# Compressing keys and values by pairs of taps over all 128 rows, with the positions' share prepared in layer 0

## The chip, the cores and the metric

The kernel runs on one core of a Trainium2 chip. The metric is the device time of one execution in microseconds (us); lower is better.

## The reference

Two layers of a decoder trunk on 256 tokens of width 1024: layer 0 mixes tokens by two sparse attentions, layer 1 by an attention with three branches; each layer then has cross-attention into 256 memory tokens and a SwiGLU feed-forward part. The change is about one small part of layer 1's mixer, the compressed branch:

```python
def nsa_compress(x, pos_emb, w1, w2):           # x: (1, 256, 4 groups, 64)
    n_cmp = (S - 32) // 16 + 1                  # 15 blocks
    idx = jnp.arange(n_cmp)[:, None] * 16 + jnp.arange(32)[None, :]
    blk = x[:, idx] + pos_emb[None, None, :, None, :]
    blk = blk.transpose(0, 1, 3, 2, 4).reshape(B, n_cmp, G, 32 * 64)
    return jax.nn.silu(blk @ w1) @ w2
...
    kc = rms_norm(nsa_compress(grp(kc), pos_k, w1_k, w2_k), kcmp_norm)
    vc = nsa_compress(grp(vc), pos_v, w1_v, w2_v)
```

Block n of a group covers tokens 16n to 16n+31, so it has 32 taps, each a vector of 64. Each tap has its own 64 x 64 slice of w1. The position embedding adds the same vector to all blocks: pos @ w1, 64 numbers for the keys and 64 for the values.

## The kernel before

Tokens lie in two tiles of 128 rows (t = 0, 1). All large weights are split in two fp32r halves: a raw tile of 2 x 128 rows by up to 512 columns comes by DMA from SyncE's queue (three raw buffers, `RAWS`), ScalarE or VectorE writes the high half (`move`), VectorE the low half (the `tensor_tensor` in `pusher`), both into one of six `whl` buffers (`PAIRS`). Such a pair is called a unit below. A raw buffer is filled anew when its unit has been split. TensorE takes three matmuls per product (`mm3`); the last multiplication of the feed-forward part, `fo`, uses each unit for 12 matmuls of 512 columns (2 tiles t x 2 row blocks x 3), and goes through 22 units, fo0 to fo21, accumulating in four PSUM tiles (`mm` and `po`).

The order of instructions on every engine is made when the program is built. Parts of the work are generators; `Steps` takes the next operation of the generators in the order of times that `Est`, the planner, gives them, and a lower rank goes first among operations that could start within 0.03 us. `Est` has a clock for each engine. What it knows of a transfer is what `est.note` tells it: `load` moves its clock of the queue by 1.45 us for a load of 512 columns and lets it land 2.0 us later. A matmul is taken for ready 0.5 us after its operands (`SLACK`). On the chip each engine goes through its instructions in that order and waits at each for its operands.

`load_cmp` is spawned by `ffn(0)` when all of the feed-forward part but `fo` has been given out. It takes four slots of the 36 shared places and issues twelve DMAs on SyncE's queue (eight of 128 KB for w1, two for w2, two for the positions, tile `posemb`). It tells the planner of none of them. Nothing in layer 0 reads them.

In layer 1, `ev_kc` transposes the four groups of keys and values of a tile on TensorE, so that the 64 dimensions of the keys stand in partitions 0 to 63 and those of the values in 64 to 127, and copies the result to `kvT`, token by token. `prep` transposes the positions and puts them in `kvT` as a fifth group. `compress` then runs 32 taps; a tap is two fp32 matmuls, one for keys and one for values, each 64 rows by 64 columns of weights, in opposite corners of the array, with 75 moving columns (5 groups x 15 blocks, 16 tokens apart). After every eight taps (`TAPS`) it waits in the planner's order for another matmul step. The positions' column of the result, `pb`, is the bias of the following silu. The rest of `compress` ends with `done("cmp")`, for which `attention` waits.

Tensors in the profile: `kvT` the transposed keys and values; `place` any of the shared places (w1, the feed-forward activations aT, scores, and others); `posemb` the positions; `w` is w2; `tp`, `sp`, `mm`, `po` are PSUM. Every operation of an engine is recorded on line 252, a helper. An fp32 matmul leaves two records, an fp32r matmul one.

Of the kernel before, what the change touches and what calls it, by code (L numbers as in the profile page):

```python
# [8 lines left out]
F32 = mybir.dt.float32  # L9
F32R = mybir.dt.float32r  # L10
# [5 lines left out]
P = 128  # L16
NB = 4
# [71 lines left out]
class Steps:  # L89
# [7 lines left out]
    def spawn(self, g, rank=2):  # L97
        self.n += 1
        self.new.append([rank, self.n, g, None])
# [253 lines left out]
def trunk(ctx: ExitStack, tc: tile.TileContext, I, out):  # L353
# [28 lines left out]
    def tt(o, a, b, op):  # L382

        return either(V.tensor_tensor(o, a, b, op=op), PO.tensor_tensor(o, a, b, op=op))
# [19 lines left out]
    def done(k):  # L404
        flags[k] = flags.get(k, 0) + 1

    def has(k, n=1):
        return lambda: flags.get(k, 0) >= n

    def tiny(n, name="tiny"):  # L410
        return tp.tile([P, n], F32, name=name, tag="tiny", bufs=96)
# [630 lines left out]
    w1s = {}  # L1042

    def load_cmp():
        w2 = hp.tile([P, P], F32, name="w2")
        pos = hp.tile([32, P], F32, name="posemb")
        yield PO.memset(w2, 0.0)
        w1 = []
        for j in range(4):
            w = yield from SL.get([P, 8, HD])  # L1050
            w1.append(w)
            for i, s in enumerate("kv"):
                nc.sync.dma_start(w[0][64 * i:64 * i + 64],
                                    I[f"nsa_cmp_w1_{s}"][0, 512 * j:512 * j + 512].rearrange("(t d) h -> d t h", d=HD))
        for i, s in enumerate("kv"):
            nc.sync.dma_start(w2[64 * i:64 * i + 64, 64 * i:64 * i + 64], I[f"nsa_cmp_w2_{s}"][0])
            nc.sync.dma_start(pos[:, 64 * i:64 * i + 64], I[f"nsa_cmp_pos_{s}"][0])
        w1s.update(w1=w1, w2=w2, pos=pos)
        done("cmpw")

    def mixer1():
# [1 line left out]
        kT = {}  # L1063
        vv = hp.tile([P, NT, 8, HD], F32, name="vv", tag="v8")
        gt = [hp.tile([P, G * HG, 3], F32, name=f"gt{t}") for t in range(NT)]
        kvT = hp.tile([P, G + 1, SEQ], F32, name="kvT", tag="kvT")
        kbd = hp.tile([P, G, 2, NCMP], F32, name="kbd")
        rq = {(j, t): hp.tile([P, 8], F32, name=f"rq{j}{t}") for j in range(2) for t in range(NT)}
        vbig = {}

        def prep():
            yield has("cmpw")
            yield PO.memset(kvT[:, G, 32:], 0.0)
            ps, f = yield from TP.get([P, 512])
            yield T.transpose(ps[:, :32], w1s["pos"], ident[:32, :32])
            yield V.tensor_copy(kvT[:, G, :32], ps[:, :32])
            f()
            done("kvT")

        def ev_kc(ps, free, t):  # L1080
            c, cf = yield from T2.get([P, G, 2, HD])
            yield S.activation(c, ps.rearrange("p (b g d) -> p g b d", b=2, g=G), AF.Copy, scale=(yield from root("mix1", t))[1])
            free()
            tps, f = yield from TP.get([P, 512])
            for g in range(G):
                yield T.transpose(tps[:, g * P:(g + 1) * P], c[:, g].rearrange("p a d -> p (a d)"), ident)
            yield S.activation(kvT[:, :G, t * P:(t + 1) * P], tps.rearrange("p (a b) -> p a b", a=G), AF.Copy)
            f()
            cf()
            done("kvT")  # L1090

        def compress():
            yield has("kvT", 3)
            NB = (G + 1) * NCMP
            N = G * NCMP
            w1 = w1s["w1"]
            hps, hf = yield from PV.get([P, 512])
            for tt in range(32):
                if tt % TAPS == 0 and tt:
                    yield has("mm", flags["mm"] + 1)  # L1100
                for i in range(2):
                    yield T.matmul(hps[64 * i:64 * i + 64, :NB], w1[tt // 8][0][64 * i:64 * i + 64, tt % 8, :],
                             kvT[64 * i:64 * i + 64, :, tt:tt + 16 * (NCMP - 1) + 1:16],
                             start=(tt == 0), stop=(tt == 31), tile_position=(64 * i, 64 * i))
            for w in w1:
                w[1]()
            pb = tiny(1, "pb")
            yield V.tensor_copy(pb, hps[:, N:N + 1])
            hs = tp.tile([P, N], F32, name="hs")
            yield S.activation(hs, hps[:, :N], AF.Silu, bias=pb)  # L1110
            hf()
            cps, f = yield from TP.get([P, 512])
            yield T.matmul(cps[:N, :P], hs, w1s["w2"], start=True, stop=True)
            kc2 = tp.tile([N, 2, HD], F32, name="kc2")
            vc = tp.tile([N, HD], F32, name="vc")
            yield V.tensor_copy(vc, cps[:N, HD:P])
            sq = tp.tile([P, HD], F32, name="sqc", tag="sqk", bufs=2)
            ss = tiny(1, "ssc")
            yield S.activation(sq[:N], cps[:N, :HD], AF.Square, accum_out=ss[:N])
            yield V.tensor_scalar(ss[:N], ss[:N], 1.0 / HD, EPS, op0=OP.mult, op1=OP.add)  # L1120
            rk = tiny(1, "rkc")
            yield from pow_half(rk[:N], ss[:N])
            yield V.tensor_scalar(kc2, cps[:N, None, :HD].to_broadcast([N, 2, HD]), rk[:N], None, op0=OP.mult)
            f()
            yield PO.memset(kbd, 0.0)
            kps, f = yield from TP.get([P, 512])
            yield T.transpose(kps[:, :N], kc2.rearrange("p a b -> p (a b)"), ident[:N, :N])
            for i in range(2):
                yield V.tensor_scalar(kbd[64 * i:64 * i + 64, :, i, :],
                                kps[64 * i:64 * i + 64, :N].rearrange("p (g n) -> p g n", g=G),  # L1130
                                kv[64 * i:64 * i + 64, 4:5], None, op0=OP.mult)
            f()

            M = 8 * NCMP
            for j in range(2):
                vbig[j] = yield from SL.get([P, 8, HD])
                vb = vbig[j][0]
                sel = tp.tile([N, 2, HG, NCMP], F32, name="sel", tag="sel")
                yield PO.memset(sel, 0.0)
                yield PO.affine_select(sel, sel, pattern=[[-NCMP, 2], [0, HG], [-1, NCMP]], compare_op=OP.not_equal,  # L1140
                                 fill=1.0, base=-2 * j * NCMP, channel_multiplier=1)
                vps, f = yield from TP.get([P, 512])
                yield T.matmul(vps[:M, :HD], sel.rearrange("p a b c -> p (a b c)"), vc, start=True, stop=True)
                vt = tp.tile([M, HD], F32, name="vt", tag="vt")
                yield V.tensor_copy(vt, vps[:M, :HD])
                f()
                yield PO.affine_select(vb[:M], vt[:, None, :].to_broadcast([M, 8, HD]),
                                 pattern=[[-NCMP, 8], [0, HD]], compare_op=OP.is_ge, fill=0.0, base=0,
                                 channel_multiplier=1)
                yield PO.affine_select(vb[:M], vb[:M], pattern=[[NCMP, 8], [0, HD]], compare_op=OP.is_ge,  # L1150
                                 fill=0.0, base=NCMP - 1, channel_multiplier=-1)
            done("cmp")
# [157 lines left out]
                                    kT[e, g][1]()  # L1310

        h = [hsel(t) for t in range(NT)]
        spawn(prep())
        spawn(compress())
        spawn(attention())
        for t in range(NT):
# [44 lines left out]
        return lambda k: tuple(mT[k // 2][e][0][:, k % 2, t * P:(t + 1) * P] for e in range(2))  # L1361

    def mem_k(L):
        kT = [hp.tile([P, MH, SEQ], F32R, name=f"mkT{e}") for e in range(2)]
        mkv[L, "k"] = kT

        def ev(ps, free, t):
            q, qf = yield from T2.get([P, MH, MD])
            yield S.activation(q.rearrange("p h d -> p (h d)"), ps, AF.Copy)
            rk = tiny(MH, "mrk")  # L1370
            yield has("mr", 1 + t)
            yield from inv_rms(ps, MH, MD, mvr[t][0], 1.0 / MD, 1.0, rk, free)
            yield V.tensor_tensor(q, q, rk[:, :, None].to_broadcast([P, MH, MD]), op=OP.mult)
            tps, f = yield from TP.get([P, 512])
            for i in range(MH):
                yield T.transpose(tps[:, i * P:(i + 1) * P], q[:, i, :], ident)
            tv = tps.rearrange("p (a b) -> p a b", a=MH)
            hi, lo = (kT[e][:, :, t * P:(t + 1) * P] for e in range(2))
            yield move(hi, tv, kv[:, 5 + L:6 + L])
            yield V.scalar_tensor_tensor(lo, tv, kv[:, 5 + L:6 + L], hi.bitcast(F32), op0=OP.mult, op1=OP.subtract)  # L1380
            f()
            qf()
            done(("mk", L))
        for t in range(NT):
            yield from gemm((L, "mk"), t, msel(t), KD, ev, pairs(("mT", L)))
# [253 lines left out]
```

## Time and profile before

| | |
|---|---|
| median of 3 runs | 785.92 us (784.57 to 786.65) |
| the profiled execution | 785.81 us |
| its span, first to last instruction | 784.0 us |
| TensorE busy | 757.2 us, 97% of the span |
| VectorE, ScalarE, GpSimd busy | 531.3, 435.7, 122.7 us |
| mean granted TensorE clock | 0.995 |

The profiled execution's own time is the span and 1.81 us around it. TensorE is busy in nearly all of the span; in the page's forty slices it is below 9 tenths in four of the first five (from 0 to 98 us) and in the last. TensorE's busy time says nothing about how fast its matmuls run.

### The profile page before, as it was taken

How to read it: one execution, taken by the hardware profiler on the slowest of the kernel's cores; microseconds unless marked ns; L12 is line 12 of the kernel's file. 1: busy time of each engine (PE TensorE's matmuls, PEld its weight loads, DVE VectorE, ACT ScalarE, POOL GpSimd, SP SyncE). 2: the span in 40 equal slices, each digit the busy share in tenths (PEclk: the TensorE clock that was granted, in tenths of full speed). 3: DMA queues.
4: the chain of work that ended last, by engine and by line, in shares of the span. 5: the costliest groups of instructions: out<-in, count | busy, mean ns of one | idle time of the engine just before them, and what ended most of it. 6: DMA issues, size and time to landing. Idle time of an engine off the chain costs nothing.

```text
span 784.0 us, 11770 instructions
## 1 busy us (share of the span) xinstructions
PE 757.2 (97%) x4227; PEld 629.6 (80%) x4227; DVE 531.3 (68%) x1111; ACT 435.7 (56%) x819; POOL 122.7 (16%) x169
## 2 busy tenths in 40 slices
PE   6898899999999999999999999999999999999998
PEld 5777687798888888878788787887888888889886
DVE  6899998778655545555717889978767546546542
ACT  5677786566545444344525889846656444444440
POOL 1554430210000000000106365301200000000000
PEclk9999899999999999999999999999999999999999
DMA  6735424435465554777524723034435566546761
GB/s 213 207 101 162 147 96 159 164 108 168 156 210 179 164 185 122 203 243 229 172 58 129 219 77 110 14 122 163 160 115 167 162 201 188 165 130 214 221 184 54
DMA packets 70635, 122.32 MB, mean 156 GB/s; under 512 B 8549, under 2 KB 15793, under 8 KB 70577
## 3 DMA queue, kind: packets, MB, share of 16 engines
q1 hardware_dynamic: 70544, 121.58, 49.7%
q8 instruction: 33, 0.54, 0.3%
q14 instruction: 26, 0.20, 0.1%
q0 software_dynamic: 32, 0.00, 0.0%
HBM read 120.51 MB, written 1.05 MB: 155 GB/s over the span
## 4 chain that ended last, share of the span: by engine, by line
PE 73%; DVE 10%; DMA 6%; ACT 4%; POOL 3%; issue 3%; SPq 1%; ACTq 0%; POOLq 0%; DVEq 0%
PE mm L252 56%; PE po L252 9%; PE tp L252 6%; DVE whl L252 3%; DMA raw<-in_ffn_w_out 3%; PE sp L252 3%; DVE place L252 3%; ACT whl L252 2%; ACT place L252 2%; DMA raw<-in_nsa_w_in 2%; POOL rope L252 1%; DMA raw<-in_ab_w_in 1%; POOL place L252 1%; DVE hss L252 1%; DMA raw<-in_nsa_w_out 1%
## 5 line engine op out<-in xcount | busy, mean ns | idle before, releaser
L252 PE MATMUL mm<-whl,h 128*128 128x512 f32 (+3 forms) x1776 | 400.4, 379 | 3.6 <-DVE whl L252 3.2
L252 DVE TENSOR_TENSOR whl<-raw,whl 128x1024 fp32r<-128x1024 f32 (+3 forms) x232 | 272.2, 1180 | 135.6 <-ACT whl L252 133.4
L252 PEld LDWEIGHTS mm<-whl,h 128*128 128x128 f32 x1776 | 310.5, 189 | 60.8 <-DVE whl L252 4.1
L252 ACT ACTIVATE whl<-raw 128x1024 fp32r<-128x1024 f32 (+3 forms) x216 | 218.3, 1012 | 193.0 <-PE mm L252 75.4
L252 PE MATMUL mm<-whl,place 128*128 128x512 f32 (+1 forms) x840 | 195.3, 376 | 0.9 <-DVE x L252 0.8
L252 PEld LDWEIGHTS mm<-whl,place 128*128 128x128 f32 x840 | 143.4, 190 | 28.2 <-DVE x L252 1.6
L252 PE MATMUL po<-whl,place 128*128 128x512 f32 x264 | 68.1, 395 | 0.0
L252 ACT ACTIVATE place<-tp 128x512 f32<-128x512 f32 (+4 forms) x115 | 54.7, 500 | 20.9 <-PE tp L252 20.4
L252 PEld LDWEIGHTS po<-whl,place 128*128 128x128 f32 x264 | 49.4, 188 | 11.4
L252 PE MATMUL tp<-ident,place 128*128 128x128 f32 (+1 forms) x340 | 53.1, 276 | 4.7 <-POOL place L252 2.3
L252 PEld LDWEIGHTS tp<-ident,place 128*128 128x128 f32 (+1 forms) x340 | 40.1, 140 | 13.9 <-issue 3.5
L252 ACT ACTIVATE place<-place,mx 128x128 f32<-128x128 f32 (+1 forms) x96 | 42.9, 453 | 7.7 <-DVE mx L252 6.6
L252 POOL TENSOR_TENSOR place<-place,rc 128x512 f32<-128x512 f32 (+2 forms) x33 | 29.7, 900 | 41.2 <-DVE rc L252 29.0
L252 POOL TENSOR_TENSOR rh<-vh,mhalf 128x1 f32<-128x1 f32 x12 | 9.9, 826 | 148.5 <-DVE vh L252 132.2
L252 ACT ACTIVATE h<-place 128x512 fp32r<-128x512 f32 x23 | 14.4, 628 | 33.0 <-DVE place L252 33.0
L252 DVE TENSOR_TENSOR x<-mm,x 128x512 f32<-128x512 f32 x36 | 24.5, 684 | 10.3 <-PE mm L252 10.2
L252 DVE CUSTOM_DVE_ANT_0 place<-sp,cm,rq 128x128 f32<-128x128 f32 (+1 forms) x80 | 30.3, 407 | 1.3 <-PE sp L252 1.2
L252 ACT ACTIVATE place<-mm 128x512 f32<-128x512 f32 (+2 forms) x45 | 23.0, 553 | 14.3 <-PE mm L252 14.3
L252 ACT ACTIVATE place<-mm,rh 128x512 f32<-128x512 f32 (+1 forms) x26 | 17.0, 654 | 22.4 <-PE mm L252 22.4
L252 DVE SCALAR_TENSOR_TENSOR place<-mm,rh,place 128x512 f32<-128x512 f32 (+1 forms) x24 | 16.9, 704 | 18.1 <-PE mm L252 18.1
L252 POOL TENSOR_TENSOR h<-place,h 128x512 fp32r<-128x512 f32 x1 | 1.3, 1294 | 175.9 <-ACT h L252 175.9
L252 PE MATMUL sp<-place,place 128*128 128x256 f32 x160 | 27.1, 300 | 0.0
(202 smaller groups left out, 620.4 us busy)
## 6 DMA issues: line engine op xcount, KB each, us to landing
raw<-in_ffn_w_in SPq DMA_DIRECT2D x80, 512.0 KB, 4.3
raw<-in_ffn_w_out SPq DMA_DIRECT2D x44, 512.0 KB, 4.3
raw<-in_ab_w_in SPq DMA_DIRECT2D x16, 512.0 KB, 4.1
raw<-in_mem_w_kv SPq DMA_DIRECT2D x16, 512.0 KB, 3.9
raw<-in_nsa_w_in SPq DMA_DIRECT2D x16, 512.0 KB, 4.1
raw<-in_ab_w_out SPq DMA_DIRECT2D x8, 512.0 KB, 3.8
raw<-in_mem_w_q SPq DMA_DIRECT2D x8, 512.0 KB, 4.0
raw<-in_mem_w_o SPq DMA_DIRECT2D x8, 512.0 KB, 4.1
```

What stands on the lines that cost most here:

```text
L252: return f(*a, **{q: v() if q in ("start", "stop") and callable(v) else v for q, v in k.items()})
```

## The change

The weights of w1 are loaded so that the 64 rows of tap j and the 64 rows of tap j + 16 stand above each other in 128 partitions, once for the keys and once for the values. `kvT` becomes two tiles, one for keys and one for values, ordered by tap within 16 tokens; each holds its own tokens in one half of the partitions, and the same tokens moved on by one block of 16 in the other. The other half is copied by a DMA on ScalarE's queue from SBUF to SBUF, when both token tiles are there. A matmul then does two taps at once: 128 rows, 64 columns of weights, 60 moving columns; keys and values go to columns 0 to 63 and 64 to 127 of the array. That is 16 x 2 matmuls instead of 32 x 2. The two new tiles share the space of the memory keys (`mkT`).

The positions' share is no column any more. It is made in `load_cmp`, in layer 0: positions loaded in four DMAs and transposed on TensorE, multiplied with w1 (four tensor operations of 128 x 512), added up (two additions, two reductions over the taps), and the two halves of the partitions added by one matmul with a column of ones; `pb` is kept. `load_cmp` now tells the planner that w1 and the positions land 8.0 us of TensorE's clock after their issue.

```diff
     def load_cmp():
         w2 = hp.tile([P, P], F32, name="w2")
         pos = hp.tile([32, P], F32, name="posemb")
+        pT = hp.tile([P, 2, 16], F32, name="posT")
+        red = hp.tile([P, 2, HD], F32, name="posw")
+        pb = hp.tile([P, 1], F32, name="posb")
         yield PO.memset(w2, 0.0)
         w1 = []
-        for j in range(4):
-            w = yield from SL.get([P, 8, HD])
-            w1.append(w)
-            for i, s in enumerate("kv"):
-                nc.sync.dma_start(w[0][64 * i:64 * i + 64],
-                                    I[f"nsa_cmp_w1_{s}"][0, 512 * j:512 * j + 512].rearrange("(t d) h -> d t h", d=HD))
+        for i, s in enumerate("kv"):
+            for j in range(2):
+                w = yield from SL.get([P, 8, HD])
+                w1.append(w)
+                for b in range(2):
+                    d0 = HD * (16 * (b ^ i) + 8 * j)
+                    nc.sync.dma_start(w[0][64 * b:64 * b + 64], I[f"nsa_cmp_w1_{s}"][0, d0:d0 + 512].rearrange("(t d) h -> d t h", d=HD))
+                est.note(w[0], est.wr, clk["PE"] + 8.0, "D")
         for i, s in enumerate("kv"):
             nc.sync.dma_start(w2[64 * i:64 * i + 64, 64 * i:64 * i + 64], I[f"nsa_cmp_w2_{s}"][0])
-            nc.sync.dma_start(pos[:, 64 * i:64 * i + 64], I[f"nsa_cmp_pos_{s}"][0])
-        w1s.update(w1=w1, w2=w2, pos=pos)
+            for b in range(2):
+                nc.sync.dma_start(pos[16 * i:16 * i + 16, 64 * b:64 * b + 64], I[f"nsa_cmp_pos_{s}"][0, 16 * (b ^ i):16 * (b ^ i) + 16])
+        est.note(pos, est.wr, clk["PE"] + 8.0, "D")
+        ps, f = yield from TP.get([P, 512])
+        yield T.transpose(ps[:, :32], pos, ident[:32, :32])
+        yield V.tensor_copy(pT.rearrange("p a b -> p (a b)"), ps[:, :32])
+        f()
+        for i in range(2):
+            u = []
+            for j in range(2):
+                u.append((yield from SL.get([P, 8, HD])))
+                yield tt(u[j][0], w1[2 * i + j][0], pT[:, i, 8 * j:8 * j + 8, None].to_broadcast([P, 8, HD]), OP.mult)
+            yield tt(u[0][0], u[0][0], u[1][0], OP.add)
+            u[1][1]()
+            yield V.tensor_reduce(red[:, i], u[0][0].rearrange("p t h -> p h t"), axis=AX.X, op=OP.add)
+            u[0][1]()
+        ps, f = yield from TP.get([P, 512])
+        yield T.matmul(ps[:, :1], red.rearrange("p a b -> p (a b)"), one, start=True, stop=True)
+        yield V.tensor_copy(pb, ps[:, :1])
+        f()
+        w1s.update(w1=w1, w2=w2, pb=pb)
         done("cmpw")
...
-            yield S.activation(kvT[:, :G, t * P:(t + 1) * P], tps.rearrange("p (a b) -> p a b", a=G), AF.Copy)
+            for i in range(2):
+                r = slice(64 * i, 64 * i + 64)
+                yield S.activation(kvT[i][r, :, :, 8 * t:8 * t + 8].rearrange("p j g n -> p g n j"),
+                                   tps[r].rearrange("p (g n j) -> p g n j", g=G, n=8), AF.Copy)
...
+            if has("kvT", NT)():
+                for i in range(2):
+                    a, b = (kvT[i][64 * e:64 * e + 64].rearrange("p j g n -> p (j g n)") for e in (i, 1 - i))
+                    nc.scalar.dma_start(b[:, :-1], a[:, 1:])
+                    est.note(b, est.wr, clk["S"] + 3.0, "D")
+                done("kvT")
...
-            for tt in range(32):
-                if tt % TAPS == 0 and tt:
+            for j in range(16):
+                if j % TAPS == 0 and j:
                     yield has("mm", flags["mm"] + 1)
-                for i in range(2):
-                    yield T.matmul(hps[64 * i:64 * i + 64, :NB], w1[tt // 8][0][64 * i:64 * i + 64, tt % 8, :],
-                             kvT[64 * i:64 * i + 64, :, tt:tt + 16 * (NCMP - 1) + 1:16],
-                             start=(tt == 0), stop=(tt == 31), tile_position=(64 * i, 64 * i))
+                yield together([T.matmul(hps[64 * i:64 * i + 64, :N], w1s["w1"][2 * i + j // 8][0][:, j % 8, :],
+                                         kvT[i][:, j, :, :NCMP], start=(j == 0), stop=(j == 15), tile_position=(0, 64 * i))
+                                for i in range(2)])
...
-            pb = tiny(1, "pb")
-            yield V.tensor_copy(pb, hps[:, N:N + 1])
...
-            yield S.activation(hs, hps[:, :N], AF.Silu, bias=pb)
+            yield S.activation(hs, hps[:, :N], AF.Silu, bias=w1s["pb"])
```

`prep` goes. `tt` gives an operation to VectorE or GpSimd, whichever the planner sees finish first; `together` gives out several matmuls without anything between them.

## Rows read from the trace of the kernel before

**Rows 1.** The page's part 1: busy time of each engine.
```profile
span 784.0 us, 11770 instructions
...
PE 757.2 (97%) x4227; PEld 629.6 (80%) x4227; DVE 531.3 (68%) x1111; ACT 435.7 (56%) x819; POOL 122.7 (16%) x169
```

**Rows 2.** Busy time in stretches: length, PE, PEld, DVE, ACT, POOL, clock, DMA.
```profile
398.00:412.00 14.00, 14.00 (x151) 11.32 (x149) 0.83 (x2) 0.91 (x2) 0.00 (x0) 1.00 0.18 56
412.00:490.00 78.00, 74.83 (x543) 64.17 (x542) 68.52 (x234) 63.15 (x172) 42.77 (x61) 1.00 0.45 134
```

**Rows 3.** The chain of waits from 400 to 412 us: start, length, what.
```profile
400.31 2.18 PE po L252 x32
...
409.11 2.19 PE po L252 x32
```

**Rows 4.** Groups of instructions by form: busy time, mean ns of one record.
```profile
L252 PE MATMUL po<-place,vv 128*64 128x128 f32 x192 | 13.5, 279 | 0.9 <-ACT place L252 0.9
L252 PE MATMUL po<-kvT,place 64*64 64x75 f32 x128 | 9.0, 304 | 0.0
L252 PE MATMUL po<-place,place 120*64 120x128 f32 x64 | 4.2, 274 | 0.0
L252 PE MATMUL tp<-place,one 76*128 76x112 f32 x2 | 0.4, 304 | 1.0 <-DVE place L252 1.0
...
L252 PEld LDWEIGHTS po<-place,vv 128*64 128x64 f32 x192 | 10.2, 136 | 3.9 <-ACT place L252 3.1 <-issue 0.5
```

**Rows 5.** The timeline at the second copy of keys and values.
```profile
398.73 0.60 ACT L252 ACTIVATE kvT<-tp 128x512 f32<-128x512 f32 x1 [0.78 <-PE tp L252]
```

**Rows 6.** DMA issues: size, median us from issue to landing.
```profile
raw<-in_nsa_w_in SPq DMA_DIRECT2D x4, 256.0 KB, 2.9
out_x<-x SPq DMA_DIRECT2D x4, 256.0 KB, 2.0
...
posemb<-in_nsa_cmp_pos_k SPq DMA_DIRECT2D x1, 8.0 KB, 1.9
```

**Rows 7.** The timeline of TensorE at the start of fo0, fo3 and fo6.
```profile
319.83 1.56 PE L252 MATMUL mm<-whl,place 128*128 128x512 f32 x6
...
328.36 1.55 PE L252 MATMUL mm<-whl,place 128*128 128x512 f32 x6
...
336.68 1.96 PE L252 MATMUL mm<-whl,place 128*128 128x512 f32 x6
```

**Rows 8.** The timeline of SyncE's queue at `load_cmp`.
```profile
321.23 0.72 SPq L1053 DMA_DIRECT2D place<-in_nsa_cmp_w_k  x1
...
324.02 2.04 SPq L1053 DMA_DIRECT2D place<-in_nsa_cmp_w_k  x1
...
330.00 0.58 SPq L1057 DMA_DIRECT2D posemb<-in_nsa_cmp_pos_v  x1
330.68 33.81 SPq L444 DMA_DIRECT2D raw<-in_ffn_w_out  x16
```

**Rows 9.** The timeline of the splits of fo6 to fo10.
```profile
334.83 1.06 ACT L252 ACTIVATE whl<-raw 128x1024 fp32r<-128x1024 f32 x1 [6.94 <-DMA raw<-in_ffn_w_out]
...
335.93 3.86 DVE L252 TENSOR_TENSOR whl<-raw,whl 128x1024 fp32r<-128x1024 f32 x3 [6.78 <-ACT whl L252]
...
344.52 1.23 DVE L252 TENSOR_TENSOR whl<-raw,whl 128x1024 fp32r<-128x1024 f32 x1 [1.47 <-ACT whl L252]
```

**Rows 10.** Groups of instructions by form, VectorE and GpSimd.
```profile
L252 DVE TENSOR_TENSOR place<-place,rc 128x512 f32<-128x512 f32 x11 | 7.8, 712 | 0.1
L252 DVE TENSOR_REDUCE hss<-place 128x8 f32<-128x512 f32 x10 | 6.7, 670 | 0.3 <-ACT place L252 0.3
...
L252 POOL TENSOR_TENSOR place<-place,rc 128x512 f32<-128x512 f32 x21 | 22.2, 1058 | 28.0 <-DVE rc L252 20.7 <-ACT place L252 7.2
```

**Rows 11.** The timeline of TensorE after its first waits.
```profile
10.63 3.86 PE L252 MATMUL mm<-whl,h 128*128 128x424 f32 x10
...
16.81 5.50 PE L252 MATMUL mm<-whl,h 128*128 128x424 f32 x27 [0.20 <-DVE whl L252]
```

More of the change, by code (lines that the diff above doesn't have):

```diff
@@ L1065, in mixer1 @@
         gt = [hp.tile([P, G * HG, 3], F32, name=f"gt{t}") for t in range(NT)]
-        kvT = hp.tile([P, G + 1, SEQ], F32, name="kvT", tag="kvT")
+        kvT = [hp.tile([P, 16, G, 16], F32, name=f"kvT{i}", tag=f"mkT{i}") for i in range(2)]
         kbd = hp.tile([P, G, 2, NCMP], F32, name="kbd")
@@ L1069, in mixer1 @@
         vbig = {}
[L1071 to L1078, printed above, removed]
         def ev_kc(ps, free, t):
@@ L1090, in ev_kc @@
             done("kvT")
+            if has("kvT", NT)():
[4 more added lines that the diff above has]
+                done("kvT")
         def compress():
             yield has("kvT", 3)
-            NB = (G + 1) * NCMP
             N = G * NCMP
+            yield has("cmpw")
             w1 = w1s["w1"]
             hps, hf = yield from PV.get([P, 512])
-            for tt in range(32):
-                if tt % TAPS == 0 and tt:
+            for j in range(16):
+                if j % TAPS == 0 and j:
                     yield has("mm", flags["mm"] + 1)
-                for i in range(2):
-                    yield T.matmul(hps[64 * i:64 * i + 64, :NB], w1[tt // 8][0][64 * i:64 * i + 64, tt % 8, :],
-                             kvT[64 * i:64 * i + 64, :, tt:tt + 16 * (NCMP - 1) + 1:16],
-                             start=(tt == 0), stop=(tt == 31), tile_position=(64 * i, 64 * i))
+                yield together([T.matmul(hps[64 * i:64 * i + 64, :N], w1s["w1"][2 * i + j // 8][0][:, j % 8, :],
+                                         kvT[i][:, j, :, :NCMP], start=(j == 0), stop=(j == 15), tile_position=(0, 64 * i))
+                                for i in range(2)])
             for w in w1:
                 w[1]()
-            pb = tiny(1, "pb")
-            yield V.tensor_copy(pb, hps[:, N:N + 1])
             hs = tp.tile([P, N], F32, name="hs")
-            yield S.activation(hs, hps[:, :N], AF.Silu, bias=pb)
+            yield S.activation(hs, hps[:, :N], AF.Silu, bias=w1s["pb"])
             hf()
@@ L1312, in mixer1 @@
         h = [hsel(t) for t in range(NT)]
-        spawn(prep())
         spawn(compress())
@@ L1363, in mem_k @@
     def mem_k(L):
-        kT = [hp.tile([P, MH, SEQ], F32R, name=f"mkT{e}") for e in range(2)]
+        kT = [hp.tile([P, MH, SEQ], F32R, name=f"mkT{e}", tag=f"mkT{e}") for e in range(2)]
         mkv[L, "k"] = kT
```

## The prediction

> **What bounds the kernel now.** I read the page's busy times first: TensorE is busy for 757.2 of 784.0 us [rows 1]. So a microsecond taken from TensorE's stream, or a microsecond for which it must stand still, is a microsecond of the end, unless the stretch around it is set by something else. Then the stretches. In that of the compression, 398 to 412 us, TensorE is busy throughout while VectorE and ScalarE work 0.83 and 0.91 of 14 us and GpSimd nothing [rows 2]: nothing else moves forward, so what is saved there moves all that follows. In the next 78 us TensorE still works 74.83 and VectorE 68.52 [rows 2]: 3.2 us of waiting that a shorter compression doesn't lengthen, since all engines start on that stretch earlier by the same amount.
>
> Last I read the stretch into which the change puts new work, the start of `fo` in layer 0. TensorE goes from fo0 at 319.83 to fo6 at 336.68 without a pause that matters [rows 7]. SyncE's queue, however, is taken from 321.23 to 330.58 by the twelve issues of `load_cmp`, and only then issues raw loads again [rows 8]. ScalarE therefore waits 6.94 us for a raw tile and VectorE 6.78 us for ScalarE; the split of fo6 ends at about 337.16 (335.93 + 1.23), when TensorE wants it at 336.68 [rows 7, 9]. The lead of the splits over the matmuls is used up exactly there.
>
> **The change, part by part.**
>
> *The matmuls of the compression.* Before: four blocks of 32 records, 2.18 to 2.19 us each in the chain, together 8.76 us; that is 68 ns a record [rows 3, 4]. After: 32 matmuls, 64 records, of 64 weight columns and 128 rows in pairs side by side. The trace has that form: values times probabilities, 128 rows by 64 columns, 13.5 us for 192 records (70 ns), and with 120 rows 4.2 us for 64 (66 ns) [rows 4]. A weight load of that form is on record with 136 ns [rows 4], twice the price, so two do overlap in a pair. The 60 moving columns are fewer than those rows' 128, the kernel before has 75 at the same price, so I take 68 ns: 64 x 68 = 4.35 us. Gain 8.76 - 4.35 = 4.4 us (bounds 4.2 to 4.6).
>
> The Trainium skill (TensorE: Matmul & The Clock Gate, "Part 3: Packing small matmuls — row/col tiling") speaks against this: it says that a weight load overlaps running matmuls only if its row group differs. The new pairs share all rows. The rows just named disagree; by that rule the gain would be gone, and it is the last rival below.
>
> *Copies and the shift.* Each of the two copies of `ev_kc` (0.60 us [rows 5]) becomes two of half the rows and the same length per row, and ScalarE issues two transfers: some 2.4 us of ScalarE in a stretch where it works 0.91 of 14 us [rows 2]; nothing. Without that cover it would be those 2.4 us. `compress` now waits for the shift, 262 KB a piece. The nearest rows land in 2.0 us (256 KB out) and 2.9 us (256 KB in) after issue [rows 6]; the second issue stands some 0.6 us behind the first, so 2.6 to 3.5 us, and up to about 4.7 if both share the engines. The planner allows 3.0 + 0.5, and fills the time with other matmuls. So 0 to 1.2 us of waiting; I take 0.4. `prep` and the copy of `pb` disappear from layer 1, off the path: nothing. One matmul by a column of ones: at most the 0.4 us of the nearest row [rows 4]; I take 0.3. The transpose of the positions is only moved.
>
> *First new wait: the positions.* `load_cmp` is given out as fo0 starts in TensorE's stream. The planner is told that `posemb` lands 8.0 us later, and puts the transpose after another 0.5 us: 8.5 us into `fo`. On the chip that is 319.83 + 8.5 = 328.3, the start of fo3, which lies at 328.36 [rows 7]. There TensorE waits for the four transfers of the positions, which are issued last. Before, the last issue starts at 330.00 [rows 8]; with two issues more, 0.58 us and a gap of 0.05 each, at 331.26; landing takes 1.9 us [rows 6]: 333.2. TensorE, which runs in order, stands for 333.2 - 328.36 = 4.8 us (4.4 to 5.2). Behind the transpose stand all further matmuls of `fo`.
>
> *Second new wait: the sum over the positions.* VectorE gets a copy (0.2), three multiplications or additions per half, and a reduction per half; the planner gives one multiplication to GpSimd by its own costs, so five operations of 0.71 and two of 0.67 us are VectorE's [rows 10]. The one on GpSimd takes about 1.06 us [rows 10] beside them. Then TensorE's matmul by ones needs the result. What matters is where these stand in VectorE's queue. The planner counts neither the twelve nor the fourteen issues as time on SyncE's queue, so for it raw tiles land every 1.45 us and the splits run up to five units ahead (six pairs). By its clocks the split of fo6 is given out before the copy, and those of fo7 to fo10 among the following operations, while the matmul by ones comes about 2 us into fo6 of TensorE's stream. On the chip the split of fo6 is late: 337.16 before [rows 9], 338.4 with the two issues more. From there VectorE has 0.2 + 5 x 0.71 + 2 x 0.67 = 5.1 us of the new work and four splits of 1.23 us, 4.9 us, in front of the matmul: 338.4 + 10.0 = 348.4. fo10's split before ran from 344.52 to 345.75 [rows 9], so with 1.26 us of shift and a raw buffer that is freed late it may itself hold the chain a little; I take 348.9 (bounds 347.1, if the second reduction stands ahead of fo10's split, and 349.6). TensorE would come there at 333.2 + 8.5 + 2 = 343.7; it waits another 5.2 us. Before, it passed this place at 336.68 + 2.06 = 338.7 [rows 7]. Both waits together: 348.9 - 338.7 = 10.2 us (8.4 to 10.9). The second depends on the first: a longer first wait makes the second shorter by as much, since the chain on VectorE sets the end.
>
> *The clock.* After the first 10 us of the kernel, in which TensorE waited for its inputs most of the time, ten matmuls took 3.86 us, later ones of the same shape 204 ns [rows 11]: half speed, 1.2 instead of 2.4 GHz, and 1.8 us lost. Two pauses of 5 us may bring that again; what falls between the two is hidden by the second. 0 to 1.8 us; I take 0.9.
>
> The same page of the Trainium skill ("Why this matters for your kernels") warns that idle gaps between bursts of matmuls put the engine back to half its clock; no row here shows a pause of that length in the middle of dense matmuls.
>
> **The sum**, against the profiled execution's own 785.81 us (784.0 and 1.81 around it; the median of the runs, 785.92, is the same): 785.8 - 4.4 + 0.4 + 0.3 + 10.2 + 0.9 = 793.2 us. With all bounds 789.5 to 796.5.
>
> **The rivals.**
>
> 1. *Only the first wait.* If the new operations stand ahead of the late splits in VectorE's queue, or the splits are not late any more because TensorE has stood still, the matmul by ones finds its operand. Then 785.8 - 4.4 + 0.7 + 4.8 = 786.9 us. For it: the first wait gives the splits 4.8 us. Against it: in-order queues, and a split of fo6 that can't end before 338.4.
>
> 2. *The waits don't come, the change is faster.* If the planner's 8 us are enough, because the positions land by 328.4 or the transpose stands later in the stream, the gain of the compression is left: 785.8 - 4.4 + 0.7 = 782.1. It decides at a landing before 328.4, and everything in the queue would have to be 4.8 us quicker than the twelve issues in the trace; or the transpose would have to be three units later. For it: one issue takes 2.04 us instead of some 0.65 [rows 8], a pause of 1.4 us that may fall away.
>
> 3. *The pairs don't overlap.* The weight loads of a pair follow one another, as the rule above has it: 64 x 136 ns = 8.7 us [rows 4], nothing gained, with both waits 797.6 us. The change's matmuls would then do no more than before. Against it: the same form at 66 to 70 ns.
>
> **How the numbers follow.** Both waits, 793.2: 0.62, own range 789.5 to 796.5. Only the first, 786.9: 0.13. No wait, 782.1: 0.18. No overlap, or a wait more that I don't see, about 797.6: 0.07. A measurement of this kernel tells differences over 0.3%, 2.4 us, from none: below 783.5 faster, above 788.3 slower. The second case falls within the bound, the third on the fast side; a few hundredths of the first reach down to it. Slower 0.67, same 0.14, faster 0.19. For 8 times in 10 the range takes the first two cases and part of both outer ones: 783 to 798 us.
>
> **What would show it.** In the profile after: 64 records of the form 128 x 64 on `kvT` (or `mkT`) in two blocks of about 2.2 us; a wait of TensorE for `posemb` of 4 to 5 us at the transpose near 328.4, and one of 3 to 6 us at the matmul by ones near 344, both in the list of waits; SyncE's queue back at raw loads at about 331.9 instead of 330.68; VectorE's new operations between the splits of fo6 and fo10. The stretch from the start of fo0 to the end of `fo` is longer by some 10 us, that of the compression shorter by some 4. The prediction is wrong if the transpose of the positions starts without a wait, if the matmul by ones does, or if the records on `kvT` take 136 ns each.

## The result, and the profile after

The kernel got slower: 790.16 us, median of 6 runs (786.70 to 793.15), against 784.54 us for the kernel before in 6 runs on the same chip; ratio 1.0066 [1.0046, 1.0086]. The profiled execution, 788.48 us, is one of the cheaper ones: the six executions range over 6.5 us, and the shorter ones have the higher mean clock (0.996 at 786.70, 0.985 and 0.991 at 792.11 and 793.15; of the kernel before, 28 later executions had 0.997 on average). So the profile shows 2.7 us of the 5.6.

Part 1 of the page after, against [rows 1]: TensorE works 7.0 us less, and the span is 2.7 us longer.

```profile
span 786.7 us, 11670 instructions
...
PE 750.2 (95%) x4165; PEld 623.7 (79%) x4165; DVE 536.7 (68%) x1124; ACT 437.1 (56%) x817; POOL 125.6 (16%) x167
```

TensorE's waits between 318 and 395 us, that is in `fo` of layer 0 (us in total, times, longest). Both waits that the prediction names are there, and no other.

```profile
PE tp L252 <- DMA posemb<-in_nsa_cmp_pos_v: 4.5, 1, 4.5
PE tp L252 <- DVE posw L252: 3.0, 1, 3.0
```

The timeline of that stretch (start, length, engine; in brackets the idle time before and what ended it), against [rows 7 to 9]:

```profile
318.96 1.56 PE L252 MATMUL mm<-whl,place 128*128 128x512 f32 x6
...
327.50 0.39 PE L252 MATMUL mm<-whl,place 128*128 128x512 f32 x1
...
329.85 1.04 SPq L1065 DMA_DIRECT2D posemb<-in_nsa_cmp_pos_v  x2
331.00 18.81 SPq L444 DMA_DIRECT2D raw<-in_ffn_w_out  x9
...
332.38 0.28 PE L252 MATMUL tp<-ident,posemb 32*128 32x32 f32 x1 [4.49 <-DMA posemb<-in_nsa_cmp_pos_v]
...
332.59 2.50 PE L252 MATMUL mm<-whl,place 128*128 128x512 f32 x5
...
336.30 1.23 DVE L252 TENSOR_TENSOR whl<-raw,whl 128x1024 fp32r<-128x1024 f32 x1 [7.93 <-ACT whl L252]
...
337.44 0.18 DVE L252 COPY posT<-tp 128x32 f32<-128x32 f32 x1
...
344.11 1.09 PE L252 MATMUL po<-whl,place 128*128 128x512 f32 x4
...
347.05 1.02 DVE L252 TENSOR_REDUCE posw<-place 128x64 f32<-128x512 f32 x1
...
348.22 0.35 PE L252 MATMUL tp<-one,posw 128*128 128x1 f32 x2 [3.02 <-DVE posw L252]
```

The transpose stands one matmul into fo3 and waits until the positions have landed. VectorE's copy of the transposed positions stands behind the late split of fo6, so it starts 5 us after the transpose; from there to the second reduction VectorE has no pause, and four splits lie between the new operations.

The same stretch in windows of 2 us (length, PE, PEld, DVE, ACT, POOL, granted clock, DMA share, GB/s):

```profile
328.00:330.00 2.00, 0.00 (x0) 0.00 (x0) 0.36 (x1) 0.00 (x0) 0.00 (x0) 0.97 0.60 134
330.00:332.00 2.00, 0.00 (x0) 0.00 (x0) 0.00 (x0) 0.00 (x0) 0.00 (x0) 0.50 0.07 13
332.00:334.00 2.00, 1.62 (x4) 1.34 (x5) 0.00 (x0) 0.00 (x0) 0.00 (x0) 0.50 0.64 201
334.00:336.00 2.00, 2.00 (x6) 1.57 (x5) 0.00 (x0) 0.79 (x1) 0.00 (x0) 0.50 1.06 409
336.00:338.00 2.00, 2.00 (x8) 1.57 (x8) 1.67 (x3) 1.46 (x3) 0.24 (x1) 0.83 0.46 177
338.00:340.00 2.00, 2.00 (x10) 1.59 (x10) 2.00 (x3) 0.93 (x1) 1.25 (x1) 1.00 0.37 134
...
346.00:348.00 2.00, 0.00 (x0) 0.00 (x0) 2.00 (x2) 0.90 (x1) 0.00 (x0) 1.00 0.61 181
348.00:350.00 2.00, 1.78 (x9) 1.55 (x10) 1.36 (x3) 0.25 (x2) 0.00 (x0) 1.00 0.84 256
```

During the first pause the granted clock falls to 0.50, 1.2 GHz, and stays there until about 336.7, and TensorE works at about half its rate: 2.50 us for five matmuls, where six take 1.56. After the second pause, 3.0 us, it is still 1.00. The Trainium skill warns of the first case (TensorE: Matmul & The Clock Gate, "Why this matters for your kernels": idle gaps between bursts return the engine to half clock); the trace agrees with 0.50.

The compression: its chain of waits, against [rows 3, 5], and TensorE's first matmuls of it in the timeline:

```profile
406.32 1.08 ACT kvT L252
...
407.42 1.09 ACT kvT L252
...
408.53 3.66 DMA kvT<-kvT
412.19 0.14 issue
412.33 1.11 PE po L252 x30
413.44 0.67 PE mm L252 x2
414.11 1.08 PE po L252 x32
```

```profile
411.59 0.30 PE L252 MATMUL po<-kvT,place 128*64 128x60 f32 x2 [0.48 <-ACT place L252]
```

A block of 32 records takes 1.08 us, 34 ns a record. The copies take 1.08 us each (0.60 before, for twice the partitions), and the two transfers of the shift land 4.1 and 3.7 us after their issue. TensorE waits 0.4 us for the second. The 0.5 us just before, which the profile puts down to ScalarE, are most likely the wait for the first: ScalarE's operation ended 0.3 us before that matmul, and the first transfer landed at 411.50, 0.1 us before it.

Three anchors divide the span. The start of fo0 moves from 319.83 to 318.96 (-0.9). The last addition of `fo`'s result to `x`, the timeline's lines below (before, then after), moves from 384.12 to 392.11: +8.0, so `fo` is 8.9 us longer. The span ends 2.7 us later: what follows `fo` gives back 5.3.

```profile
384.12 0.68 DVE L252 TENSOR_TENSOR x<-po,x 128x512 f32<-128x512 f32 x1
...
392.11 0.68 DVE L252 TENSOR_TENSOR x<-po,x 128x512 f32<-128x512 f32 x1
```

### The profile page after: what moved, and what is told of

Read it like the earlier page. It is cut to its first block, busy times and chain, and to the rows that moved or that the text cites. A ratio compares the mean times of both kernels' runs of the same rounds, so it can differ in the third digit from the quotient of the medians.

```text
span 786.7 us, 11670 instructions
## 1 busy us (share of the span) xinstructions
PE 750.2 (95%) x4165; PEld 623.7 (79%) x4165; DVE 536.7 (68%) x1124; ACT 437.1 (56%) x817; POOL 125.6 (16%) x167
## 4 chain that ended last, share of the span: by engine, by line
PE 70%; DVE 13%; DMA 6%; issue 3%; ACT 3%; POOL 3%; SPq 1%; ACTq 0%; DVEq 0%; POOLq 0%
PE mm L252 54%; PE po L252 9%; PE tp L252 5%; DVE whl L252 4%; DVE place L252 4%; PE sp L252 2%; DMA raw<-in_ffn_w_out 2%; ACT place L252 2%; DMA raw<-in_ab_w_in 1%; DMA raw<-in_ffn_w_in 1%; DMA raw<-in_nsa_w_in 1%; ACT whl L252 1%; POOL rope L252 1%; DVE rc L252 1%; DVE hss L252 1%
## 5 line engine op out<-in xcount | busy, mean ns | idle before, releaser
L252 ACT ACTIVATE whl<-raw 128x1024 fp32r<-128x1024 f32 (+2 forms) x215 | 217.3, 1012 | 205.8 <-PE mm L252 72.2
L252 POOL TENSOR_TENSOR place<-place,rc 128x512 f32<-128x512 f32 (+2 forms) x34 | 32.1, 945 | 36.1 <-DVE rc L252 24.1
L252 PEld LDWEIGHTS sp<-place,place 128*128 128x128 f32 x160 | 22.7, 193 | 3.3 <-issue 1.0
```

The lines of the kernel that those rows point to most:

```text
L252: return f(*a, **{q: v() if q in ("start", "stop") and callable(v) else v for q, v in k.items()})
```

## The experiments

Theory: the pairs are worth some 6 us, and making the constant in layer 0 loses more, by two waits in instruction order, of which VectorE's queue sets the second. The rivals: one of the waits costs all; the due time of 8 us is what is amiss; the pairs' gain comes from the missing 15 columns, not from the pairs. All diffs are against the changed kernel unless said otherwise.

| kernel | us (range, runs) | ratio to before |
|---|---|---|
| the change | 790.16 (786.70 to 793.15, 6) | 1.0066 [1.0046, 1.0086] |
| positions loaded first | 790.76 (788.73 to 792.81, 6) | 1.0068 [1.0049, 1.0086] |
| due in 14 us | 791.89 (789.49 to 792.64, 5) | 1.0071 [1.0057, 1.0085] |
| ones in layer 1 | 785.81 (783.95 to 787.37, 12) | 1.0001 [0.9990, 1.0012] |
| late work | 784.88 (781.42 to 787.89, 12) | 0.9988 [0.9971, 1.0005] |
| column | 780.20 (778.08 to 786.27, 11) | 0.9940 [0.9923, 0.9958] |
| column, loads later | 782.26 (780.63 to 782.68, 5) | 0.9951 [0.9938, 0.9965] |
| constant, loads spread | 781.79 (779.62 to 782.42, 6) | 0.9948 [0.9934, 0.9963] |
| column, loads spread | 778.38 (777.96 to 779.73, 4) | 0.9911 [0.9897, 0.9924] |

**Positions loaded first.** The loads of w2 and of the positions go ahead of w1's:

```diff
         yield PO.memset(w2, 0.0)
+        for i, s in enumerate("kv"):
+            nc.sync.dma_start(w2[...], I[f"nsa_cmp_w2_{s}"][0])
...
+        est.note(pos, est.wr, clk["PE"] + 8.0, "D")
         w1 = []
...
```

> The changed kernel, with w2 and the positions issued ahead of the eight transfers of w1. Theory (the end of both waits is set by VectorE's queue, whose new operations stand behind the late split of fo6): the wait for posemb is gone, the wait for posw grows from 3.0 to some 7 or 8 us and ends at about the same time, and the whole is within 2 us of the changed kernel. Rival (two waits with a price each): the wait for posw stays at 3 us, and 4 to 5 us are won.

The wait for the positions is gone, and the other one is longer; from the list of TensorE's waits:

```profile
PE tp L252 <- DVE posw L252: 8.2, 1, 8.2
```

8.2 in place of 4.5 + 3.0. The matmul by ones starts 28.7 us after fo0, 29.3 in the change, and the medians are the same. So the waits don't add: VectorE's queue sets the end.

What comes behind that end is not the same. A window around it, with the clock:

```profile
340.00:362.00 22.00, 13.78 (x50) 10.79 (x49) 13.85 (x15) 7.30 (x7) 0.12 (x1) 0.77 0.61 191
```

A mean of 0.77 over 22 us is some 10 us at 0.50. They outlast the wait: the fourteen matmuls behind it take 5.8 us, where fourteen take 3.3 at full clock, and `fo` takes 75.3 us, 73.2 in the profile of the change.

**Ones in layer 1.** The matmul by a column of ones, which needs the sum over the positions, moves to the head of `compress`:

```diff
-        ps, f = yield from TP.get([P, 512])
-        yield T.matmul(ps[:, :1], red.rearrange("p a b -> p (a b)"), one, start=True, stop=True)
-        yield V.tensor_copy(pb, ps[:, :1])
...
         def compress():
...
+            yield T.matmul(ps[:, :1], w1s["red"].rearrange("p a b -> p (a b)"), one, start=True, stop=True)
+            yield V.tensor_copy(w1s["pb"], ps[:, :1])
```

> The changed kernel with only the matmul by ones moved to layer 1; the transpose and the products stay where they are. Theory: the wait for posemb stays at 4.5 us and still brings half clock, now hidden by nothing; the wait for posw is gone; the whole 1 to 4 us under the changed kernel, 785 to 789 us. If instead the first wait were free, the whole would be near 780 us.

The wait for `posw` is gone, that for the positions is 4.2 us, and the ratio is 0.65% below the change's, 5.1 us: without a reader in `fo`, VectorE's lag makes TensorE wait nowhere in `fo`.

**Late work.** The same, and the transpose and what follows it wait until step 6 of `fo`, two units to a step, that is fo12.

```diff
         est.note(pos, est.wr, clk["PE"] + 8.0, "D")
+        yield has("late")
...
+            if L == 0 and i == 6:
+                done("late")
```

> The changed kernel, with the position work (transpose, products, sums) given out later: the transpose and products when unit fo12 of layer 0's last multiplication is reached, the matmul by ones in layer 1 just ahead of the compression. Transfers and their order are unchanged. Theory (the loss is two waits of TensorE, which runs in order, and the half clock after them): no wait for posemb or posw in layer 0, the stretch from fo0 to the last sum of that multiplication, 64.3 us before and 73.2 after, is back at 64 to 66 us, the whole about 779 us, 5 to 6 us under the kernel before. Rival (the new work itself slows the splits wherever it stands, by 5 us of VectorE): the stretch stays above 70 us and the whole at or above the kernel before.

Half missed: neither wait is there, but `fo` took 69.6 us, not 64 to 66, and the whole 784.88, not 779. Three waits came in their place, in the list of TensorE's waits from 318 to 392 us and in two windows:

```profile
PE tp L252 <- DVE x L252: 2.8, 1, 2.8
PE mm L252 <- DVE whl L252: 0.8, 1, 0.8
PE mm L252 <- ACT whl L252: 0.6, 1, 0.6
```

```profile
333.00:338.00 5.00, 3.64 (x15) 2.45 (x14) 1.35 (x2) 2.12 (x2) 0.00 (x0) 1.00 0.85 306
378.00:383.00 5.00, 4.13 (x15) 3.40 (x16) 2.19 (x4) 0.63 (x1) 1.28 (x1) 0.73 0.56 173
```

At 333 to 338 TensorE stands 1.4 us for splits: the gap in the raw loads that the fourteen issues leave, which the first wait had covered. Up to 379 it waits 2.8 us for the residual sum. VectorE's new work had ended at 368.5; the sum stands behind two splits of layer 1's weights, for whose raw tiles ScalarE waits 1.8 and 1.4 us. How the later place of the new work led to that is not shown.

**Column.** The constant goes; the positions stand as a 65th moving column in `kvT`, put there in layer 1 as before.

```diff
-        kvT = [hp.tile([P, 16, G, 16], F32, name=f"kvT{i}", tag=f"mkT{i}") for i in range(2)]
+        kvT = [hp.tile([P, 16, 16 * G + 1], F32, name=f"kvT{i}", tag=f"mkT{i}") for i in range(2)]
...
+        def prep():
...
+            for i in range(2):
+                yield V.tensor_copy(kvT[i][:, :, 16 * G], w1s["pT"][:, i])
```

> The pairs of taps alone: the positions are a 65th moving column, put in place in layer 1, and no position work is left in layer 0; the fourteen transfers stay. Theory: no wait in layer 0, the compression as cheap as in the change (records of about 35 ns instead of 68), the whole about 779 to 780 us, 5 us under the kernel before. Rival (the constant is what makes the compression cheap): records near 68 ns and the whole about as before.

780.20 us, 0.60% under before: the pairs without the constant are a gain. The profile is that of the slowest of the eleven executions, 786.27 us (the others 778.08 to 782.48); in it TensorE waits 2.1 us in `fo` for splits. A block of 32 in the timeline, with 65 columns here and with 60 in the change:

```profile
409.34 1.15 PE L252 MATMUL po<-kvT,place 128*64 128x65 f32 x32
...
414.04 1.15 PE L252 MATMUL po<-kvT,place 128*64 128x60 f32 x32
```

Leaving the column away saves the compression nothing.

**Taps not alternating** (one run, 789.12 us; before beside it 786.14). A block's eight key matmuls (sixteen records) come first, then its eight for the values.

```diff
-            for j in range(16):
-                if j % TAPS == 0 and j:
+            for j0 in range(0, 16, TAPS):
+                if j0:
...
-                                for i in range(2)])
+                                for i in range(2) for j in range(j0, j0 + TAPS)])
```

> The changed kernel with the matmuls of a block in another order: eight taps of the keys, then eight of the values, instead of keys and values in turn. If the price of 34 ns a record comes from the two column halves working side by side, the records take 50 to 68 ns and a block of 32 some 1.6 to 2.2 us instead of 1.1. If one weight load behind another is what costs 34 ns in any order, the blocks stay at 1.1 us.

The chain of waits:

```profile
411.45 1.82 PE po L252 x32
...
413.93 1.82 PE po L252 x32
```

57 ns a record in place of 34, at a clock of 1.00 in both: side by side they do overlap.

**Before with 60 columns** (one run, 784.18 us, against the kernel before; the positions' share is left out of the result).

```diff
-            NB = (G + 1) * NCMP
+            NB = G * NCMP
...
-                             kvT[64 * i:64 * i + 64, :, tt:tt + 16 * (NCMP - 1) + 1:16],
+                             kvT[64 * i:64 * i + 64, :G, tt:tt + 16 * (NCMP - 1) + 1:16],
...
-            yield S.activation(hs, hps[:, :N], AF.Silu, bias=pb)
+            yield S.activation(hs, hps[:, :N], AF.Silu)
```

> The kernel before with 60 instead of 75 moving columns in the compression: the positions' share is left out (neither computed nor added). If the records of the opposite corners are priced by their moving columns, 68 ns falls to about 55 (75 to 60 columns) and a block of 32 from 2.19 to about 1.75 us. If they are priced by the weight load, the block stays at 2.19 us.

The chain of waits, four blocks, of which two:

```profile
399.94 1.78 PE po L252 x32
...
407.53 1.79 PE po L252 x32
```

56 ns a record, 68 with 75 columns [rows 3]: in this form a record's price goes by its moving columns (60/75 of 68 is 54). Dropping columns saves the kernel before 1.6 us of TensorE. The rest of the gain comes with the new form: half as many records, at 34 ns in place of 56.

**Corners not alternating** (one run, 792.8 us; the kernel of the last experiment, so the positions' share is left out here too; a block's keys first, then its values).

```diff
-                for i in range(2):
+                for i, tt in [(i, tt) for i in range(2) for tt in range(t0, t0 + TAPS)]:
```

> As e6 (the kernel before with 60 moving columns, the positions' share left out), with eight taps of the keys and then eight of the values instead of keys and values in turn. If matmuls in opposite corners of the array do not work side by side, the order makes no difference and a block of 32 records stays at 1.79 us. If they do, the block gets longer, as that of the change did without alternating (1.08 to 1.82 us).

The chain of waits, and windows over it:

```profile
400.34 3.04 PE po L252 x32
...
411.78 1.58 PE mm L252 x3
413.35 3.24 PE po L252 x32
```

```profile
400.00:403.40 3.40, 3.40 (x35) 2.97 (x33) 0.00 (x0) 0.00 (x0) 0.00 (x0) 1.00 0.28 89
403.40:407.00 3.60, 3.60 (x34) 3.25 (x34) 0.00 (x0) 0.00 (x0) 0.00 (x0) 0.63 0.00 0
407.00:412.00 5.00, 5.00 (x36) 4.14 (x37) 0.00 (x0) 0.00 (x0) 0.00 (x0) 0.50 0.00 0
```

The first block, at full clock, takes 3.04 us, 95 ns a record in place of 56. So opposite corners overlap too when they alternate. The later blocks are at half clock. There three matmuls of 512 columns take 1.58 us (0.90 with the corners alternating), but a block of one corner at a time takes only 7% more, 3.24 us: its price is not set by TensorE's clock. What sets it is open. One thing that differs beside the rows is the order of `kvT`: here the moving columns lie 16 tokens apart, in the change next to each other, and no run separates that from the pairs.

**Due in 14 us.** The planner is told the landing of w1 and of the positions 6 us later:

```diff
-        est.note(pos, est.wr, clk["PE"] + 8.0, "D")
+        est.note(pos, est.wr, clk["PE"] + 14.0, "D")
```

> The changed kernel with the planner told that w1 and the positions land 14.0 instead of 8.0 us after their issue, which is what the profile shows. Theory (the first wait is a false due time, the second the lag of VectorE's queue behind the planner, which grows with how far the splits run ahead): the wait for posemb is gone, the wait for posw stays, some 3 to 8 us, and the whole is 0 to 4 us under the changed kernel, above 785 us. Rival (the false due time is the whole fault): both waits are gone and the whole is near 780 us.

Missed: the wait for the positions is gone, that for `posw` is again 8.2 us, and the ratio is no lower than the change's. The due time explains only the first wait.

**Column, loads later.** The column's kernel, with `load_cmp` spawned at layer 1's mixer and due in 14 us:

```diff
         h = [hsel(t) for t in range(NT)]
+        spawn(load_cmp())
         spawn(prep())
...
-        if L == 0:
-            spawn(load_cmp())
```

> The column version (e3_column) with all fourteen transfers of the compression given out at the start of layer 1 instead of the start of fo in layer 0. Theory (the fourteen issues hold the raw loads back for 10 us, and the splits' lead is used up at fo6 in every version that has them there): no wait of TensorE from fo0 to the last sum, that stretch at 64 us or a little under, where the profile of e3_column has 67; the whole 1 to 3 us under e3_column, 777 to 779 us. Rival: in layer 1 the same issues hold back the raw loads there, and TensorE waits for splits or for w1 instead; then the whole is at 780 us or above.

`fo` has no wait (62.8 us), but TensorE then stands 2.0 us in each of the next two windows, where it worked 20.00 and 18.80 us in the version with spread loads:

```profile
380.00:400.00 20.00, 18.02 (x87) 14.32 (x86) 12.81 (x22) 13.19 (x22) 1.11 (x2) 1.00 0.68 179
400.00:420.00 20.00, 18.08 (x154) 14.76 (x153) 11.23 (x39) 8.11 (x20) 5.98 (x9) 1.00 0.46 124
```

The cost had moved, not gone: the mixer of layer 1 has loads of its own, and VectorE waits 3.7 us for one of its raw tiles behind the fourteen issues.

**Constant, loads spread, and column, loads spread.** `load_cmp`'s issues are spread over the first six steps of `fo`, two units to a step: one of w1's four tiles with each of the first four, w2 and the positions with the next two; the first on the change as it is, the second on the column's kernel.

```diff
+                yield has(("foi", 0), 1 + 2 * i + j)
                 w = yield from SL.get([P, 8, HD])
...
+            yield has(("foi", 0), 5 + i)
             nc.sync.dma_start(w2[...], I[f"nsa_cmp_w2_{s}"][0])
...
             yield has(("aT", L, i), 2)
+            done(("foi", L))
```

> The changed kernel with its transfers spread over fo in the same way; the position work follows the last of them, planned 8.0 us after it. Theory: the wait for posemb is gone (six transfers in two short rows land long before 8 us); the wait for posw shrinks to 0 to 5 us, since the splits are no longer held back by ten microseconds of issues but still run less far ahead than the planner has it; the whole 781 to 787 us, above e9. If the row of issues had nothing to do with the lag, the wait would stay at 8 us and the whole near 790 us.

> The column version (e3_column) with its transfers spread over fo: two w1 transfers with each of the first four steps of two units, w2 and the positions with the next two, instead of fourteen in a row. Theory (what is left to win in layer 0 is the late split of fo6, whose cause is the row of issues on one queue): no wait of TensorE in fo, none moved into layer 1 as in e7, the whole 0 to 3 us under e3_column, 777 to 780 us. If the raw loads of fo are at the rate of the transfers anyway, a wait comes back elsewhere in fo and nothing is won.

With the constant 781.79 us: the waits shrink to 0.5 us for the positions and 1.7 us for `posw`. With the column 778.38 us, 0.89% under before, the fastest kernel here; TensorE has no pause in `fo`:

```profile
320.00:384.00 64.00, 64.00 (x284) 51.63 (x283) 35.70 (x40) 27.46 (x31) 1.83 (x2) 1.00 0.76 215
```

## Why the prediction was right

The time lies in the range, and the likeliest case, both waits, is the one that came. The sum was too high, by 3.0 us for the median, which lies in that case's own range, 789.5 to 796.5, and by 4.7 for the profiled execution, which lies under it. (Its terms' bounds add up to 789.6 to 795.9.) That the median is the nearer one is luck: it holds time at lower clocks that the sum does not have. The terms one by one, with times counted from the start of fo0, which lies 0.9 us earlier in the profile after:

- *The compression: mis-sized.* Forecast -4.4 us (bounds 4.2 to 4.6) at 68 ns a record; the blocks take 1.11 + 1.08 us, say 2.2 to 2.3 with the two records that stand apart, so -6.5 at 34 ns. The step that failed is "the kernel before has 75 [columns] at the same price, so I take 68 ns". In opposite corners the price goes by moving columns (56 and 68 ns at 60 and 75), and the two forms differ. A nearer row was there: values times probabilities [rows 4] alternate between column halves too, over 128 rows, and 70 ns x 60/128 is 33. That scaling is rough: 60 and 65 columns cost the same.
- *The first wait: right.* 4.5 us at the start of fo3, 4.8 forecast.
- *The second wait's end: right.* 29.3 us after fo0, 29.1 forecast. Its length, 3.0 and not 5.2, follows from TensorE's arrival, 26.2 and not 23.9 us after fo0: at half clock eleven matmuls took 4.5 us from 332.59 on, where eleven take 2.6.
- *What both waits cost: 9.5 us, with the half clock between them, and not 10.2.* The matmul by ones stands ten matmuls into fo6. Before, the tenth is the fourth of the six in the first line below and ends at 339.58, 19.8 us after fo0; the forecast put this place at 338.7.
- *The clock: counted double.* In the profiled execution the half clock lies between the two waits and is hidden by the second, as the text said; the 0.9 us on top was not there. The row behind the term [rows 11] shows slow matmuls alone: the windows of the kernel before give a clock of 1.00 from 10 to 14 us. In the profile with the positions first half clock did cost time, behind the second wait. Three of the other five executions of the change have a mean clock as low as that one's, 0.989, or lower, but no profile shows where they lose it.
- *Overlooked:* before, TensorE waited 0.9 us for `x` at the end of `fo` (second line below); after, it has no wait there. 9.5 and 0.35 for the matmul by ones, less these 0.9, are the 8.9 us by which `fo` is longer.
- *The shift wait: 0.4 forecast, 0.9 measured* if the first transfer's wait is counted, within the bounds 0 to 1.2. *The copies*, 1.08 us each, were put at nothing; they stand in the chain ahead of the shift, and cost TensorE no more than these 0.9. *The ones:* 0.35 us, 0.3 forecast.

```profile
338.48 1.56 PE L252 MATMUL po<-whl,place 128*128 128x512 f32 x6
...
PE tp L252 <- DVE x L252: 0.9, 1, 0.9
```

From the profiled execution before, the forecast was +7.4 us. The profile has +2.7: 0.9 less before fo0, 2.5 less in `fo` (8.9 for 11.4), 1.3 more gained after it (5.3 for 4.0). The change alters nothing before fo0: around 93 us the clock is at 0.50 for 6.8 us in the profile before and for 3.4 us in that after, so these 0.9 us are a difference between two executions.

The third rival, that the pairs don't overlap, falls: it needed 136 ns a record, and pairs over the same 128 rows take 34 ns alternating and 57 not. The Trainium skill's rule in TensorE: Matmul & The Clock Gate, "Part 3: Packing small matmuls — row/col tiling", that a weight load overlaps running matmuls only if its row group differs, is not borne out by this trace. Another page of the Trainium skill, TensorEngine Tiling (Array Packing), "Key Properties", says that different tiles load weights and multiply in parallel; with that the 34 ns agree.

What the experiments show of the loss: taking only the first wait away gains nothing (two kernels; the second wait grows to 8.2 us in both), taking the second's reader out of `fo` gains 5.1 us, taking the constant out 9.9 us, and spreading the issues 9.3 us with the constant kept (each from its ratio and the change's). It is argued and not shown why spreading shortens `posw`'s wait: the splits are then less late, but VectorE's order changes with them.

## What to carry to other kernels

Price a small matmul from the row that is nearest in its placement in the array and in how its moving columns lie, and take a scaling by columns for an estimate; a new form can be worth more than the columns saved. Work that fills an idle engine is not free if an in-order engine that sets the end reads its result soon after: let the reader stand where the operand is old. And count DMA issues as time of the queue that makes them, since fourteen in a row hold back every load behind them by 10 us.

## What the runs showed of the hardware that I had not expected

- Pairs of 128 rows by 64 columns cost 34 ns a record at 60 and at 65 moving columns when they alternate between column halves, 57 ns when not (60 columns); opposite 64 x 64 corners 56 and 95 ns at 60. One corner at a time, a block took 3.04 us at a clock of 1.00 and 3.24 at 0.50. Why a 64-row matmul alone costs more than a 128-row one is left open; the moving columns lay apart in the one and side by side in the other.
- The granted clock fell from 1.00 to 0.50 with corners not alternating, in a stretch in which TensorE was busy throughout, and was back at 1.00 from 422 us on. A clock that falls is no proof of a pause. Nor did the length of a pause tell: after the 3.0 us of the change's second wait the clock was 1.00, after the 2.8 us in the kernel with late work it fell (0.73 on average from 378 to 383 us).
- A ScalarE copy of 512 elements a row takes 1.08 us when it scatters its output by taps, 0.60 us when it writes in order. The reduction over taps, read across, takes 1.02 to 1.06 us, where one over adjacent elements took 0.67 [rows 10]; the two also differ in their outputs, 64 and 8 a row.
